# Seven products for a seventh pair, one weight sum by an adding DMA, and separate rooms, in a one-core encoder layer

## The chip, the cores and the metric

The kernel runs on one core of one Trainium2 chip. The metric is device time in microseconds (us): the time of one execution, as the median of several. A profiled execution also has a span, from its first to its last instruction.

The engines are PE (TensorE: matmuls, with PEld for the loads of its stationary operand), DVE (VectorE), ACT (ScalarE), POOL (GpSimd) and SP (SyncE). Almost all DMAs are issued from SP; DMAs that add what they bring to what lies at the destination are issued from POOL. Weights and activations are in float32.

## What the kernel computes

One layer of an encoder on 256 tokens of width 2048:

```python
h = x + 0.5 * rms_norm(swiglu(rms_norm(x, g1), w_gate1, w_up1, w_down1), p1)   # first FFN
u = rms_norm(h, g2); q, k, v, f, g = split(u @ w_in)
    # grouped-query attention on q, k, v (16 heads, 4 kv heads); a 2-D Fourier mix of f; gates from g
merged = sigmoid(g_A) * (attention @ w_attn_o) + sigmoid(g_B) * (fourier(f) @ w_fourier)
h = h + rms_norm(merged @ w_out, p2)
y = h + 0.5 * rms_norm(swiglu(rms_norm(h, g3), w_gate2, w_up2, w_down2), p3)   # second FFN

def swiglu(x, w_gate, w_up, w_down):
    return (silu(x @ w_gate) * (x @ w_up)) @ w_down
```

`w_gate` and `w_up` are 2048 x 5632 and `w_down` is 5632 x 2048; the two FFNs hold most of the arithmetic. The output has the shape of the input, in float32.

## The kernel before

**One product in three matmuls.** Every float32 operand is cut in two parts, `hi` (ACT copies it into a reduced format, L104) and `lo` (DVE subtracts `hi` from the source, L105). `mm3` (L108) multiplies two cut operands in three matmuls: hi by hi, lo by hi, hi by lo (L110 to L112). So each weight costs a load from HBM, an ACT copy and a DVE subtraction of the same size before PE may use it. "Split" below means this pair of instructions. A weight piece is 128 x 1024 (two rows of tiles of 128 x 512).

**The FFN.** The hidden width of 5632 is done in 11 blocks of 512 (`ffn`, L710). The first two blocks (`PLAIN` = 2) are straight products (`col_block`). The other nine go through `swiglu` (L558): the 16 tiles of the contraction, each 128 deep, are taken as eight pairs, and the 256 tokens are two tiles of 128. One pair has four activation tiles (two token tiles by two contraction tiles) and four weight tiles (gate and up, each by two contraction tiles): a 2 x 2 by 2 x 2 block product. Straight, this is eight products, 24 matmuls. By Strassen's scheme it is seven products of sums, 21 matmuls. `BY_SEVEN` (L48) names the pairs that go by seven: 0, 1, 2, 4, 5 and 6. Pairs 3 and 7 are straight.

**Left and right factors.** The seven left factors (sums of activation tiles) are made once for each FFN in `Forms.chunk` (L480) and kept. The right factors are sums of weights that are new for every block, and DVE makes them in `seven` (L602):

```python
minus(t[:, 0, :], ra[:, 1, :], ra[:, 0, :])           # L616; pairs in RAW_B8: one of 1024, L613
minus(t[:, 1, :], rb[:, 0, :], ra[:, 1, :])
b = ring(rb[:])                                       # split of 1024
minus(ra[:, 1, :], rb[:, 0, :], t[:, 0, :])           # L620
b = ring(h["t"][:])                                   # second(): split of 1024
minus(h["t"][:, 0, :], h["ra"][:, 1, :], h["rb"][:, 1, :])
line.feed(lambda: ring(h["ra"][:]), ...)              # split of 1024
line.feed(lambda: ring(h["t"][:, 0:1, :]), ...)       # split of 512
```

All subtractions go through the helper at L582. The sums after the products (`add`, L584, with its instruction at L587) put the seven accumulators together once in a block: eight additions and, at L599, two multiplications by the activated gate. `row_line` (L662) then multiplies a finished block by its rows of `w_down` (96 matmuls) while the next block is fed.

**The line and the ring.** `Line` (L525) is a hand-written order. `feed` appends a piece and, unless a piece with `hold` has stopped it, at once writes its preparation (load and split); `next` writes the matmuls of the oldest piece. So preparation runs up to `RING + RING_B8` = 8 pieces ahead of the matmuls, in split buffers (the ring): six in pool `wring` and two in `b8`. On DVE, ACT and PE this order is the order of execution. The order on SP and POOL is chosen by a scheduler at build time.

**Rooms.** Pool `b8` has 12 rooms of 8 KB per partition: left factors, two ring pieces, the raw 1 MB loads of pairs 0, 2, 4 and 6 (`RAW_B8`), layer inputs `u`, sums `y`, residual `h`, gains and the attention operands. Other raw pieces use five rooms of `wraw`. Pool `chunk` has three rooms for each of hi and lo of the hidden activations and serves as scratch.

**Handover and end.** `last_rows` (L261) does the last rows of a stage, then its norm (`PostNorm`) and the transposes of the next stage's input. The norm needs a reciprocal root, done on DVE in ten small instructions (`rsqrt_steps`, L151).

**Adding DMAs.** Two of four column groups of each `row_line` are added into `y` by a POOL DMA (L702), and the 16 pieces of the Fourier weights are folded by one each (L928).

Of the kernel before, what the change touches and what calls it, by code (L numbers as in the profile page):

```python
# [39 lines left out]
QSCALE = HD ** -0.5  # L40

# [17 lines left out]
def encoder_layer(  # L59
# [14 lines left out]
    b8 = pool("b8", B8)  # L74
    chunk = pool("chunk", CH)
# [11 lines left out]
    def big(name, dt=F32, shape=None):  # L87
        return b8.tile(shape or [P, D], dt, tag="b8", name=name)
# [38 lines left out]
    def pieces(src, spare=None):  # L127
# [4 lines left out]
        def part(k0):  # L132
            if spare in (None, "chunk"):
                return piece(src, k0, WP, (chunk, "ch_hi", "ch_lo") if spare else None)
            if not whole:
                for c in ("h", "l"):
                    shape = [P, CK, NB]
                    whole[c] = big("w" + c, F32R, shape)
# [12 lines left out]
    def rsqrt_steps(ssq, n, inv, name, mult=1.0, pre=None):  # L151

        up = (8.0 / 3.0 / mult) ** 2
        a, y, t, w, q, z, t2, w2, r = (small(name + c, n) for c in "aytwqzuvr")
        i = sm.tile([P, n], I32, tag="smi" + str(n), name=name + "i")
# [4 lines left out]
        yield r, V.tensor_scalar(out=i[:], in0=a[:].bitcast(I32), scalar1=1, scalar2=None, op0=ALU.logical_shift_right)  # L160
        yield r, V.tensor_scalar(out=y[:].bitcast(I32), in0=i[:], scalar1=-1.0, scalar2=float(0x5F3759DF),
                                 op0=ALU.mult, op1=ALU.add)
        yield r, V.tensor_tensor(out=t[:], in0=y[:], in1=y[:], op=ALU.mult)
        yield r, V.tensor_tensor(out=w[:], in0=t[:], in1=a[:], op=ALU.mult)
        yield r, V.scalar_tensor_tensor(out=q[:], in0=w[:], scalar=-10.0 / 3.0, in1=w[:], op0=ALU.add, op1=ALU.mult)
        yield r, V.scalar_tensor_tensor(out=z[:], in0=q[:], scalar=5.0, in1=y[:], op0=ALU.add, op1=ALU.mult)
        yield r, V.tensor_tensor(out=t2[:], in0=z[:], in1=z[:], op=ALU.mult)
        yield r, V.scalar_tensor_tensor(out=w2[:], in0=t2[:], scalar=-0.5 * 9.0 / 64.0, in1=a[:],
                                        op0=ALU.mult, op1=ALU.mult)
        yield r, V.scalar_tensor_tensor(out=r[:], in0=w2[:], scalar=1.5, in1=z[:], op0=ALU.add, op1=ALU.mult)  # L170
# [16 lines left out]
    def new_u(t):  # L187
        return tuple(big(f"u{c}{t}", F32R, [P, KD, P]) for c in "hl")
# [164 lines left out]
    def bcast(src, name):  # L353
        g = big(name)
        load(g[:], src.partition_broadcast(P))
        return g
# [4 lines left out]
    class PostNorm:  # L361
# [26 lines left out]
        def sums(self, t):  # L388
            up = (8.0 / 3.0 / self.half) ** 2
# [117 lines left out]
    def ring(src):  # L507
# [3 lines left out]
        if turn["more"] and i % 4 == 1:  # L511
            both = big("w2", F32R, [P, 2, WP, NB])
# [45 lines left out]
    def swiglu(line, forms, w, hs, behind={}):  # L558
# [4 lines left out]
        def mul(n, a, b, last=False):  # L563
            if n not in ps:
                ps[n] = ptr.tile([P, NB], F32, tag="tr", name="pc") if n in ("p5", "p7", "p1") else                     pmm.tile([P, NB], F32, tag="mm", name="pc")
            mm3(ps[n][:], *a, *b, n not in begun, last)
            begun.add(n)
# [4 lines left out]
        def plain(pair, i, *then, hold=False):  # L572
            def use(b):
                for t in range(NT):
                    for j in range(2):
                        k = 2 * pair + j
                        mul("gu"[i] + str(t), forms.plain[k][t], b[j], k == KD - 1)
# [3 lines left out]
        def minus(out, a, b):  # L581
            V.tensor_tensor(out=out, in0=a, in1=b, op=ALU.subtract)  # L582

        def add(out, a, b):  # L584
            if out not in x:
                x[out] = work(out)
            V.tensor_tensor(out=x[out][:], in0=ps[a][:], in1=x[b][:], op=ALU.add)  # L587
# [5 lines left out]
        def silu(t):  # L593
            g = x["x" + "13"[t]]
            A.activation(g[:], g[:], AF.Silu)

        def times(t):
            g, up = x["x" + "13"[t]], x["x" + "25"[t]]
# [3 lines left out]
        def seven(pair, between=None, *then):  # L602
# [4 lines left out]
            def first():  # L607
                t = chunk.tile([P, WP, NB], F32, tag=("ch_hi", "ch_lo")[BY_SEVEN.index(pair) % 2], name="t13")
                if turn["more"] and pair in RAW_B8:
                    four = big("raw4", F32, [P, 2 * WP, NB])  # L610
                    load(four[:], w[pair // 2].rearrange("p (i k c) -> p i k c", i=2, c=NB)[:, pair % 2])
                    ra, rb = four[:, 0:WP, :], four[:, WP:, :]
                    minus(t[:], four[:, 1:3, :], ra)  # L613
                else:
                    ra, rb = raw(pair, 0), raw(pair, 1)
                    minus(t[:, 0, :], ra[:, 1, :], ra[:, 0, :])  # L616
                    minus(t[:, 1, :], rb[:, 0, :], ra[:, 1, :])
                h.update(ra=ra, rb=rb, t=t)
                b = ring(rb[:])
                minus(ra[:, 1, :], rb[:, 0, :], t[:, 0, :])  # L620
                return b

            def second():
                b = ring(h["t"][:])
                minus(h["t"][:, 0, :], h["ra"][:, 1, :], h["rb"][:, 1, :])
                return b

            def two(n, a, m, b, last):
                def use(ws):
                    mul(n, a, ws[0], last)  # L630
                    mul(m, b, ws[1], last)
                return use

            line.feed(first, two("u0", s4, "g0", a12, False))
            line.feed(second, two("p5", s1, "p7", s3, end), hold=end)
            if between:
                between()
            line.feed(lambda: ring(h["ra"][:]), two("p1", a11, "p6", s2, end), *then[0:2], hold=end)
            line.feed(lambda: ring(h["t"][:, 0:1, :]), lambda ws: mul("g1", na22, ws[0]), *then[2:], hold=end)

        sums = [copy, lambda: add("x2", "p6", "x1"), lambda: add("x3", "p7", "x2"), lambda: add("x2", "p5", "x2"),
                lambda: add("x5", "p5", "x3")]
        gates = [lambda: add("x1", "g0", "x1"), lambda: add("x3", "g1", "x3"), lambda: silu(0), lambda: silu(1)]
        ups = [lambda: add("x2", "u0", "x2"), lambda: times(0), lambda: add("x5", "u1", "x5"), lambda: times(1)]
        for kg in range(KD // CK):
            a, b = 2 * kg, 2 * kg + 1
            if kg == KD // CK - 1:
                seven(a, None, *sums)
                if a in behind:
                    behind[a]()  # L650
                plain(b, 0, *gates, hold=True)
                plain(b, 1, *ups)
            elif b in BY_SEVEN:
# [4 lines left out]
            else:  # L658
                seven(a, lambda: plain(b, 0))
                plain(b, 1)  # L660

    def row_line(line, ch, w, rb, y, way, ahead):  # L662
# [4 lines left out]
        rooms = {(0, 0): (ptr, "tr"), (1, 0): (ptr, "tr"), (1, 1): (ptr, "tr")} if not first else {}  # L667
# [42 lines left out]
    def ffn(u, rs, wg, wu, wgu, wd, yname, tail, gate0, w_next=None, early=()):  # L710
# [29 lines left out]
        line = Line()  # L740
        end = []
        with tc.manual_schedule(engines={mybir.EngineType.DVE, mybir.EngineType.Activation, mybir.EngineType.PE}):
            for f in range(PLAIN, nblk + 1):
# [11 lines left out]
                if f < nblk:  # L755
                    hs = []
                    turn["more"] = True
                    swiglu(line, forms, wgu[f - PLAIN], hs, {
# [57 lines left out]
    def fourier_signs():  # L816
        alt = four["alt"] = xpool.tile([P, GROUPS // 2, NYR], F32R, tag="xt", name="alt")
        A.activation(alt[:].rearrange("p a b -> p (a b)"), constant(dft_ones[:, WE + P:], GROUPS // 2 * NYR)[:], AF.Copy)
        mid = four["mid"] = xpool.tile([NS, 2 * P + 2 * NYR], F32R, tag="xt", name="mid")
        mraw = work("mraw", [NS, 2 * P + 2 * NYR])  # L820
        load(mraw[:], dft_mid)
        A.activation(mid[:], mraw[:], AF.Copy)
# [566 lines left out]
```

## Time and profile before

| | before |
|---|---|
| median of 3 runs (lowest to highest) | 2001.39 us (2001.24 to 2002.6) |
| the profiled execution: time | 2003.93 us |
| the profiled execution: span | 2001.9 us |
| mean granted TensorE clock | 0.998 |
| PE busy | 1985.0 us (99%) |
| DVE busy | 1780.3 us (89%) |
| ACT busy | 1300.2 us (65%) |
| POOL busy | 84.4 us (4%) |
| DMA moved | 434.20 MB, mean 217 GB/s |

Busy time is the union of an engine's instructions in the records. Matmuls overlap in the records (a row lasts 0.39 us, the next one starts 0.23 us later), so a time on PE is worked out from start to start. An instruction row reads: start, duration, engine, line, operation, output<-input, shape, count and, in brackets, idle time before it with what ended that. In the rows, `wlo` or `w` from L105 is a DVE split, `pc` an accumulator of gate and up, `pr` one of the row products, `pt` a transpose. `w` alone is one of the two ring pieces in `b8`: every fourth piece.

### The profile page before, as it was taken

To read this page: it belongs to the slowest core of one execution; us is meant where nothing else is said; L and a number is where in the kernel's file an instruction comes from. 1 tells how busy PE (TensorE), PEld (TensorE's weight loads), DVE (VectorE), ACT (ScalarE), POOL (GpSimd) and SP (SyncE) were. 2 spreads that over 40 slices of the span, in tenths; PEclk is the share of its full clock that TensorE was granted. 3 is DMA by queue.
4 is the path that set the end of the run, shared out by engine and by line. 5 is a ranking of instruction groups with operands and counts; after the bars stand their busy time and mean duration, and the time that the engine had idled before them with its cause. 6 is when DMAs were issued, how large, how long until landed. Compare 5 with 4: busy or idle time off the path is not lost.

```text
span 2001.9 us, 25805 instructions
## 1 busy us (share of the span) xinstructions
PE 1985.0 (99%) x9146; PEld 1643.9 (82%) x9146; DVE 1780.3 (89%) x2352; ACT 1300.2 (65%) x1860; POOL 84.4 (4%) x94
## 2 busy tenths in 40 slices
PE   9999999999999999999999999999999999999998
PEld 7888888888888878888888888878888888888886
DVE  6999999999999888886877885878999999999996
ACT  7566766767666756556666564656677766777666
POOL 0000000000000010100000000000000000000002
PEclk9999999999999999999999999999999999999999
DMA  9657766677768796954555657565577766677683
GB/s 326 220 178 237 225 223 208 200 247 221 230 198 281 244 290 193 260 182 141 191 187 190 193 166 276 194 215 195 175 231 231 231 211 210 210 234 229 207 266 127
DMA packets 117585, 434.20 MB, mean 217 GB/s; under 512 B 12840, under 2 KB 18992, under 8 KB 106064
## 3 DMA queue, kind: packets, MB, share of 16 engines
q1 hardware_dynamic: 103888, 411.65, 60.6%
q0 software_dynamic: 13568, 20.91, 6.0%
q8 instruction: 71, 1.16, 0.2%
q14 instruction: 58, 0.48, 0.1%
HBM read 409.44 MB, written 6.29 MB: 208 GB/s over the span
## 4 chain that ended last, share of the span: by engine, by line
PE 92%; DVE 4%; DMA 2%; ACT 1%; issue 0%; SPq 0%; DVEq 0%; ACTq 0%
PE pc L111 18%; PE pc L112 18%; PE pc L110 18%; PE pr L112 10%; PE pr L111 10%; PE pr L110 10%; DVE wlo L105 2%; PE pt L180 1%; DMA raw<-in_w_fo 1%; PE pe L110 0%; PE pe L112 0%; PE pe L111 0%; DMA raw<-in_f_gu 0%; PE pt L1077 0%; PE pf L112 0%
## 5 line engine op out<-in xcount | busy, mean ns | idle before, releaser
L105 DVE TENSOR_TENSOR wlo<-raw,whi 128x1024 fp32r<-128x1024 f32 (+1 forms) x567 | 680.4, 1218 | 97.2 <-ACT whi L104 95.7
L104 ACT ACTIVATE whi<-raw 128x1024 fp32r<-128x1024 f32 (+1 forms) x567 | 586.0, 1052 | 253.9 <-PE pc L112 95.4
L111 PE MATMUL pc<-wlo,fh 128*128 128x512 f32 x738 | 287.5, 390 | 0.0
L112 PE MATMUL pc<-whi,fl 128*128 128x512 f32 x738 | 287.3, 389 | 0.0
L110 PE MATMUL pc<-whi,fh 128*128 128x512 f32 x738 | 287.1, 389 | 0.0
L110 PE MATMUL pc<-whi,uh 128*128 128x512 f32 x688 | 271.8, 396 | 1.0 <-ACT uh L834 1.0
L111 PE MATMUL pc<-wlo,uh 128*128 128x512 f32 x688 | 269.8, 392 | 2.0 <-DVE wlo L105 2.0
L112 PE MATMUL pc<-whi,ul 128*128 128x512 f32 x688 | 269.8, 392 | 0.0
L104 ACT ACTIVATE whi<-t 128x1024 fp32r<-128x1024 f32 (+1 forms) x198 | 171.6, 867 | 136.7 <-DVE t L582 125.5
L582 DVE TENSOR_TENSOR t<-raw 128x512 f32<-128x512 f32 (+1 forms) x252 | 208.9, 841 | 15.0 <-DMA raw<-in_f_gu 11.1
L110 PE MATMUL pr<-whi,hTh 128*128 128x512 f32 x544 | 213.4, 392 | 0.0
L112 PE MATMUL pr<-whi,hTl 128*128 128x512 f32 x544 | 211.8, 389 | 0.0
L111 PE MATMUL pr<-wlo,hTh 128*128 128x512 f32 x544 | 211.7, 389 | 0.0
L105 DVE TENSOR_TENSOR wlo<-t,whi 128x1024 fp32r<-128x1024 f32 (+1 forms) x198 | 193.4, 977 | 13.5 <-ACT whi L104 12.8
L104 ACT ACTIVATE w<-raw 128x1024 fp32r<-128x1024 f32 x144 | 152.0, 1055 | 42.0 <-DVE raw L582 35.3
L105 DVE TENSOR_TENSOR w<-raw,w 128x1024 fp32r<-128x1024 f32 x144 | 175.5, 1219 | 0.0
L111 PEld LDWEIGHTS pc<-wlo,fh 128*128 128x128 f32 x738 | 138.5, 188 | 29.5 <-DVE wlo L105 0.3
L110 PEld LDWEIGHTS pc<-whi,fh 128*128 128x128 f32 x738 | 138.5, 188 | 29.0
L112 PEld LDWEIGHTS pc<-whi,fl 128*128 128x128 f32 x738 | 138.5, 188 | 28.9
L111 PEld LDWEIGHTS pc<-wlo,uh 128*128 128x128 f32 x688 | 129.8, 189 | 28.9 <-DVE wlo L105 3.7
L110 PEld LDWEIGHTS pc<-whi,uh 128*128 128x128 f32 x688 | 129.9, 189 | 28.2 <-ACT uh L834 2.4
L112 PEld LDWEIGHTS pc<-whi,ul 128*128 128x128 f32 x688 | 129.6, 188 | 27.2 <-DVE ul L105 0.5
(360 smaller groups left out, 3185.1 us busy)
## 6 DMA issues: line engine op xcount, KB each, us to landing
raw<-in_f_down SPq DMA_DIRECT2D x176, 512.0 KB, 5.3
raw<-in_f_gu SPq DMA_DIRECT2D x144, 512.0 KB, 4.6
raw<-in_f_gu SPq DMA_DIRECT2D x72, 1024.0 KB, 7.7
raw<-in_w_in SPq DMA_DIRECT2D x112, 512.0 KB, 4.4
raw<-in_f_up SPq DMA_DIRECT2D x32, 512.0 KB, 4.8
raw<-in_w_ao SPq DMA_DIRECT2D x32, 512.0 KB, 4.3
raw<-in_w_out SPq DMA_DIRECT2D x32, 512.0 KB, 4.5
raw<-in_f_gate SPq DMA_DIRECT2D x31, 512.0 KB, 6.0
```

The costliest lines, as they stand in the source:

```text
L104: a = A.activation(hi, src, AF.Copy)
L105: v = V.tensor_tensor(out=lo, in0=src, in1=hi.bitcast(F32), op=ALU.subtract)
L110: T.matmul(ps, lh, rh, start=first, stop=False, skip_group_check=onto)
L111: T.matmul(ps, lh, rl, start=False, stop=False, skip_group_check=onto)
L112: return T.matmul(ps, ll, rh, start=False, stop=last, skip_group_check=onto)
L180: T.transpose(pt[:, j, :], src[:, j * P:(j + 1) * P], ident[:])
L582: V.tensor_tensor(out=out, in0=a, in1=b, op=ALU.subtract)
```

## The change

- **`BY_SEVEN` takes in pair 3.** Each of the 18 blocks (nine in each FFN) has seven pairs by seven products and one straight pair.
- **Another form of the seven products.** Before the products, DVE makes two subtractions for a pair, one of 512 and one of 1024 with a repeated operand; the third sum (first up tile plus first gate tile) is made by an adding DMA. The up half of a pair is loaded from SP into a room of the new pool `half`; then POOL issues a DMA that adds the first gate tile, 256 KB, onto its first tile; the gate half is loaded as an ordinary raw piece, so that the first gate tile comes twice. Class `Sums` fetches so up to three pairs ahead.
- **Order.** The fourth piece of a pair (`late`) is fed after the first piece of the next pair. The accumulator of up for the second token tile is gone: the straight pair adds onto the product `p5`. Seven additions close a block.
- **Rooms.** `b8` has 8 rooms; `rr` 2 rooms of 8 KB (the ring's two pieces, later the second token tile of `u`); `half` 6 rooms of 4 KB (the raw pairs, gains in halves, k, v and a Fourier operand, part of the last rows' weights); `chunk` 2 instead of 3. The left factors take three rests of `xpool` instead of one, so two Fourier constants move: `alt` to `const`, `mid` to a load and a copy at the start of the mixer.
- **Roots.** On one column, seven instructions instead of ten; on four columns, nine.

The diff, cut to its core:

```diff
-RAW_B8 = (0, 2, 4, 6)
-SPARE = (None, None, "chunk", "u")
+SPARE = (None, None, "chunk", "rr")
-B8 = 12
+B8 = 8
+RR = 2
+HALF = 6
-BY_SEVEN = (0, 1, 2, 4, 5, 6)
-CH = 3
+BY_SEVEN = (0, 1, 2, 3, 4, 5, 6)
+SUMS_AHEAD = 3
+CH = 2
...
             if spare in (None, "chunk"):
-                return piece(src, k0, WP, (chunk, "ch_hi", "ch_lo") if spare else None)
+                other = (chunk, "ch_hi", "ch_lo") if k0 == 0 else (half, "half", "half")
+                return piece(src, k0, WP, other if spare else None)
...
-        yield r, V.tensor_scalar(out=i[:], in0=a[:].bitcast(I32), scalar1=1, scalar2=None, op0=ALU.logical_shift_right)
-        yield r, V.tensor_scalar(out=y[:].bitcast(I32), in0=i[:], scalar1=-1.0, scalar2=float(0x5F3759DF),
-                                 op0=ALU.mult, op1=ALU.add)
-        yield r, V.tensor_tensor(out=t[:], in0=y[:], in1=y[:], op=ALU.mult)
-        yield r, V.tensor_tensor(out=w[:], in0=t[:], in1=a[:], op=ALU.mult)
+        yield r, V.tensor_scalar(out=y[:].bitcast(I32), in0=a[:].bitcast(I32), scalar1=-0.5,
+                                 scalar2=float(0x5F3759DF - 2 ** 31), op0=ALU.mult, op1=ALU.add)
+        def square_times_a(out, t, src):
+            if n == 1:
+                yield r, V.scalar_tensor_tensor(out=out[:], in0=src[:], scalar=src[:, 0:1], in1=a[:], op0=ALU.mult, op1=ALU.mult)
+            else:
+                yield r, V.tensor_tensor(out=t[:], in0=src[:], in1=src[:], op=ALU.mult)
+                yield r, V.tensor_tensor(out=out[:], in0=t[:], in1=a[:], op=ALU.mult)
+        yield from square_times_a(w, t, y)
...
         if turn["more"] and i % 4 == 1:
-            both = big("w2", F32R, [P, 2, WP, NB])
+            both = big("w2", F32R, [P, 2, WP, NB], rr)
...
+    class Sums:
+        def __init__(self, wgu, blocks):
+            self.todo = [(wgu[f], pair) for f in range(blocks) for pair in BY_SEVEN]
+            self.ready = []
+        def fetch(self):
+            w, pair = self.todo.pop(0)
+            src = w[pair // 2].rearrange("p (q i k c) -> p q i k c", q=2, i=2, c=NB)[:, pair % 2]
+            ra = small_room("ra", F32, [P, WP, NB])
+            load(ra[:], src[:, 1])
+            nc.gpsimd.dma_start(ra[:, 0, :], src[:, 0, 0], accum_op=ALU.add)
+            self.ready.append(ra)
+        def get(self):
+            while len(self.ready) <= SUMS_AHEAD and self.todo:
+                self.fetch()
+            return self.ready.pop(0)
...
             def first():
+                a = h["a"] = sums_.get()
+                b = ring(a[:])
+                V.tensor_tensor(out=a[:, 0, :], in0=a[:, 0, :], in1=a[:, 1, :], op=ALU.subtract)
                 return b
             def second():
+                b = h["b"] = raw(pair, 0)
+                r = ring(b[:])
+                V.tensor_tensor(out=b[:], in0=h["a"][:, 0:1, :].to_broadcast([P, WP, NB]), in1=b[:], op=ALU.subtract)
+                return r
+            line.feed(first, lambda ws: (mul("p5", s1, ws[0], end), mul("u0", s4, ws[1])))
+            while late:
+                late.pop()()
+            line.feed(second, lambda ws: (mul("p1", a11, ws[0], end), mul("g0", a12, ws[1])), *then[0:1], hold=end)
+            line.feed(lambda: ring(h["a"][:, 0:1, :]), lambda ws: mul("p6", s2, ws[0], end), *then[1:3], hold=end)
+            late.append(lambda: line.feed(lambda: ring(h["b"][:]),
+                                          lambda ws: (mul("p7", s3, ws[0], end), mul("g1", na22, ws[1], end)),
+                                          *then[3:], hold=end))
...
-        rooms = {(0, 0): (ptr, "tr"), (1, 0): (ptr, "tr"), (1, 1): (ptr, "tr")} if not first else {}
+        rooms = {(0, 0): (ptr, "tr"), (1, 0): (ptr, "tr")} if not first else {}
```

The rest of the diff gives every tile its new pool and splits the loads of the gains (`Gains`, 2 x 512 KB instead of 1 MB each).

More of the change, by code (lines that the diff above doesn't have):

```diff
@@ L74, in encoder_layer @@
     b8 = pool("b8", B8)
+    rr = pool("rr", RR)
+    half = pool("half", HALF)
     chunk = pool("chunk", CH)
@@ L137, in part @@
                     shape = [P, CK, NB]
[L138 removed]
+                    whole[c] = big("w" + c, F32R, shape, rr if spare == "rr" else b8)
             raw = wraw.tile([P, WP, NB], F32, tag="raw", name="raw")
@@ L351, in last_rows, with __init__, __getitem__ @@
         return ps
[L353 to L356, printed above, removed]
+    class Gains:
+        def __init__(self, src, name):
+            self.two = [small_room(name, F32, [P, D // 2]) for _ in range(2)]
+            for i, g in enumerate(self.two):
+                load(g[:], src[:, i * D // 2:(i + 1) * D // 2].partition_broadcast(P))
+        def __getitem__(self, at):
+            i, lo = divmod(at[1].start, D // 2)
+            return self.two[i][:, lo:lo + at[1].stop - at[1].start]
     def cbs(a, cb):
@@ L593, in silu, with seven @@
         def silu(t):
-            g = x["x" + "13"[t]]
+            g = x["x" + "12"[t]]
             A.activation(g[:], g[:], AF.Silu)
         def times(t):
-            g, up = x["x" + "13"[t]], x["x" + "25"[t]]
+            g, up = x["x" + "12"[t]], x["x" + "43"[t]]
             V.tensor_tensor(out=up[:], in0=up[:], in1=g[:], op=ALU.mult)
             hs.append(up)
-        def seven(pair, between=None, *then):
+        late = []
+        def seven(pair, *then):
             a11, a12, na22, s1, s2, s3, s4 = forms.seven[pair]
@@ L607, in first @@
             def first():
[L608 to L617, printed above, removed]
@@ L628, in two @@
[L628 to L639, printed above, removed]
@@ L645, in swiglu @@
+        sums = [copy, lambda: combine("x2", "p6", "x1", ALU.add), lambda: combine("x4", "p5", "x2", ALU.subtract)]
+        gates = [lambda: combine("x3", "p7", "x2", ALU.add), lambda: combine("x2", "g1", "x3", ALU.add),
+                 lambda: silu(0), lambda: silu(1)]
+        ups = [lambda: combine("x4", "u0", "x4", ALU.add), lambda: times(0),
+               lambda: combine("x3", "p5", "x3", ALU.subtract), lambda: times(1)]
         for kg in range(KD // CK):
@@ L647, in swiglu @@
             if kg == KD // CK - 1:
-                seven(a, None, *sums)
+                seven(a, *sums, *gates)
                 if a in behind:
                     behind[a]()
-                plain(b, 0, *gates, hold=True)
+                plain(b, 0, lambda: combine("x1", "g0", "x1", ALU.add), hold=True)
+                late.pop()()
                 plain(b, 1, *ups)
-            elif b in BY_SEVEN:
+            else:
                 seven(a)
@@ L894, in norm_rope @@
         return o
-    dps, dcs, odd, first, alt, mid = (four[n] for n in ("dps", "dcs", "odd", "first", "alt", "mid"))
-    kT = big("kT", F32R, [P, 2, 4, S])
-    vs = big("vs", F32R, [P, 2, NT, NB])
+    dps, dcs, odd, first, alt = (four[n] for n in ("dps", "dcs", "odd", "first", "alt"))
+    mm_ = xpool.tile([NYR, 3 * P + 2 * NYR], F32R, tag="xt", name="mid")
+    mid, mids = mm_[0:NS, 0:2 * P + 2 * NYR], mm_[:, 2 * P + 2 * NYR:]
+    mraw = work("mraw", [NS, 2 * P + 2 * NYR])
+    load(mraw[:], dft_mid)
+    kT = [small_room("kT" + c, F32R, [P, 4, S]) for c in "hl"]
+    vs = [small_room("vs" + c, F32R, [P, NT, NB]) for c in "hl"]
     ueo = [[big(f"u{n}{c}", F32R, [P, KD, P]) for c in "hl"] for n in "eo"]
@@ L1168, in encoder_layer @@
     kro = []
-    gate(10, mB, 0, between=[lambda b=b: fold_tokens(b) for b in range(1, 4)]
+    gate(10, mB, 0, between=[lambda b=b: fold_tokens(b) for b in range(1, 4)] + [lambda: A.activation(mid, mraw[:], AF.Copy)]
          + [lambda t=t: kro.append(norm_rope(pk, "k", t)) for t in range(NT)])
```

86 lines of the change are left out of this document (34 added, 52 removed).

## The prediction

> **What bounds the kernel now.** I read the page first, then the busy time of each engine by stretches, then the matmuls of one block of the FFN in order of time.
>
> ```profile
> span 2001.9 us, 25805 instructions
> PE 92%; DVE 4%; DMA 2%; ACT 1%; issue 0%; SPq 0%; DVEq 0%; ACTq 0%
> 174.61 0.87 PE pt L180 x8
> 236.84 0.87 PE pt L180 x8
> 270.20 0.39 PE L110 MATMUL pc<-w,fh 128*128 128x512 f32 x1
> 274.96 0.39 PE L110 MATMUL pc<-w,fh 128*128 128x512 f32 x1
> ```
>
> The chain that ended last is PE for 92% of the span. The transposes that come once in a block start 236.84 - 174.61 = 62.23 us apart: that is a block's period. The two matmuls each begin the piece of a pair that lies in one of the ring's special rooms, one pair (21 matmuls) apart: 4.76 / 21 = 0.2267 us for a matmul, whatever its row's 0.39 us says. A block has 6 x 21 + 2 x 24 + 96 = 270 matmuls, 61.2 us; with the transposes it fills the period. So PE runs at its own pace here, and a matmul less is 0.2267 us less, as long as the operands come.
>
> ```profile
> core 0: us, PE busy (x) PEld busy (x) DVE busy (x) ACT busy (x) POOL busy (x), PEclk, DMA share, GB/s
> 236.80:299.10 62.30, 62.30 (x281) 51.58 (x280) 60.42 (x69) 42.57 (x54) 3.52 (x5) 1.00 0.69 218
> 610.20:660.00 49.80, 49.80 (x224) 41.26 (x223) 48.00 (x56) 31.16 (x38) 0.92 (x2) 1.00 0.80 276
> 660.00:720.00 60.00, 58.55 (x273) 47.50 (x272) 51.18 (x84) 41.70 (x76) 4.39 (x4) 1.00 0.80 266
> ```
>
> Beside a full PE, DVE is busy 60.42 of 62.30 us. It is the second bound, with 1.9 us to spare, and whether a block gets shorter depends on whether DVE's work shrinks with PE's.
>
> **The matmuls.** Pair 3 goes from 24 matmuls to 21, in nine blocks of two FFNs: 18 x 3 x 0.2267 = 12.24 us. The new period would be 61.55 us. The new form of the products still has seven, and the straight pair, the row products and the transposes stay.
>
> **DVE's work.** Six rows give the subtractions, the additions and the pace.
>
> ```profile
> L582 DVE TENSOR_TENSOR t<-raw 128x512 f32<-128x512 f32 x180 | 121.1, 689 | 3.7
> L582 DVE TENSOR_TENSOR t<-raw 128x1024 f32<-128x1024 f32 x72 | 87.8, 1220 | 11.3 <-DMA raw<-in_f_gu 11.1
> L582 DVE TENSOR_TENSOR raw<-raw,t 128x512 f32<-128x512 f32 x108 | 73.9, 684 | 0.0
> L587 DVE TENSOR_TENSOR x<-pc,x 128x512 f32<-128x512 f32 x144 | 92.5, 683 | 1.2
> L486 DVE TENSOR_TENSOR un<-un,r 128x1024 f32<-128x1024 f32 x8 | 9.7, 1221 | 0.1
> 265.71 1.22 DVE L105 TENSOR_TENSOR w<-raw,w 128x1024 fp32r<-128x1024 f32 x1
> 266.84 0.68 DVE L105 TENSOR_TENSOR wlo<-t,whi 128x512 fp32r<-128x512 f32 x1
> 267.45 1.22 DVE L582 TENSOR_TENSOR t<-raw 128x1024 f32<-128x1024 f32 x1
> ```
>
> Start to start, an instruction of 1024 takes 266.84 - 265.71 = 1.13 us and one of 512 takes 0.61 us. By the counts, divided by 18, a block now has 10 + 6 = 16 subtractions of 512, four of 1024, and eight additions. Afterwards it has seven of 512, seven of 1024 and seven additions. Replacing a straight pair takes two splits of 1024 away and brings three of 1024 and one of 512. Net: of 1024, -4 + 7 - 2 + 3 = +4; of 512, -16 + 7 - 1 + 1 = -9. That is 4 x 1.13 - 9 x 0.61 = -0.97 us: DVE needs about 59.5 us in 61.55 and keeps 2.1 us to spare. The subtraction with a repeated operand is costed at 1.13 us because L486, with a repeated operand too, has the same 1221 ns as the plain ones. ACT gains one copy of 1024 and one of 512, bounded above by the 1.22 and 0.68 us of DVE's rows for the same sizes, so at most 1.9 us on 42.57: covered.
>
> **DVE's lead.** Within the sevens DVE is slower than PE, and lives on the lead it has won in the row products.
>
> ```profile
> 265.44 0.39 PE L110 MATMUL pc<-w,fh 128*128 128x512 f32 x1
> 259.17 1.22 DVE L105 TENSOR_TENSOR w<-raw,w 128x1024 fp32r<-128x1024 f32 x1
> 272.18 1.22 DVE L105 TENSOR_TENSOR w<-raw,w 128x1024 fp32r<-128x1024 f32 x1
> 254.39 1.23 DVE L582 TENSOR_TENSOR t<-raw 128x1024 f32<-128x1024 f32 x1 [0.54 <-DMA raw<-in_f_gu]
> ```
>
> The splits that end at 260.39, 266.93 and 273.40 are used at 265.44, 270.20 and 274.96: the lead goes from 5.05 to 3.27 to 1.56 us, about 1.75 us lost in a pair, since DVE takes 6.5 us for a pair and PE 4.76. The new form has one instruction of 512 less in such a pair: 5.9 us, a loss of 1.13. Now six pairs lose 10.5 us and the straight pair 3 gives back 24 x 0.2267 - 2 x 1.13 = 3.2, together 7.3; afterwards seven pairs lose 7.9 with nothing in between. The smallest lead goes from 1.56 to about 1.0 us, or 1.6 if the closing addition that DVE saves counts fully towards it. It stays above zero, so I cost it at nothing; if it is used up, each us that is missing in a block is 18 us in the end.
>
> **DMA, SP and POOL.** Each pair by seven now also moves 256 KB through an adding DMA.
>
> ```profile
> DMA  9999868048976204860576000588989986998799
> GB/s 294 390 278 192 191 221 287 18 79 311 387 248 248 87 0 79 316 279 0 161 242 253 18 0 0 169 279 269 248 242 348 453 348 161 316 306 229 308 383 229
> DMA packets 3518, 13.79 MB, mean 222 GB/s; under 512 B 394, under 2 KB 394, under 8 KB 3001
> q1 hardware_dynamic: 2885, 12.60, 59.5%
> q0 software_dynamic: 629, 1.14, 10.1%
> raw<-in_f_gu SPq DMA_DIRECT2D x144, 512.0 KB, 4.6
> y<-part POOLq DMA_DIRECT2D x32, 256.0 KB, 7.5
> DMA to landing us min/median/max: 6.4/7.9/12.1
> L702 POOL DMA_DIRECT2D y<-part x32: 847/941/1215, 168.2 to 610.3; - x32
> ```
>
> These are the DMAs of the block from 174.6 to 236.8 us, in 40 slices, and the nearest price of an adding DMA: POOL's sums onto `y`. In this block they cost 0.101 x 16 x 62.2 / 1.14 = 88 us of engine time for each MB; seven times 0.262 MB add 162 us to 0.70 x 16 x 62.2 = 697. That is 859 of 16 x 61.55 = 985 us, a share of 87%. The rate would be (13.79 + 1.83) / 61.55 = 254 GB/s, less than the 276 GB/s of the stretch from 610.2 us, where PE had no gap. So I take the throughput as sufficient. New waits: POOL's add waits for the up half to land, with later adds and the row products' sums queued behind it; ACT's split of the sum waits for the add, with all splits, and DVE, behind it; SP's load waits for a room of `half`, with the raw loads behind it. One sum needs 4.6 us to load, 0.94 to issue and 7.9 (12.1 at worst) to land: 13.4 to 17.6 us. Six rooms are 28.6 us of PE at 4.76 a pair, and about 6 us of that a room is in use, so 22 us are there. POOL goes from four issues in a block to eleven, 10.3 us of 61.55. These cost nothing on the path; their upper bound is the second rival.
>
> **The rest.** Three steps of the root go. At the end of the kernel nothing covers them:
>
> ```profile
> 1993.36 0.15 DVE L160 TENSOR_SCALAR ci<-ca 128x1 int32<-128x1 int32 x1
> 1993.55 0.15 DVE L161 TENSOR_SCALAR cy<-ci 128x1 int32<-128x1 int32 x1
> 1993.73 0.48 DVE L163 TENSOR_TENSOR ct<-cy 128x1 f32<-128x1 f32 x1
> 1994.26 0.16 DVE L164 TENSOR_TENSOR cw<-ct,ca 128x1 f32<-128x1 f32 x1
> ```
>
> A step is 0.19 us from start to start, the third row 0.53. Three steps are 0.57 us, 0.91 if the long one goes; I take 0.57. At the two handovers the same 0.57 us lies on a path where PE has up to 1.45 us of gaps (660 to 720 us): a gain between 0 and 1.1, and I count 0. Against it, the smaller pools can hold things up: with two rooms in `chunk`, the last rows' third weight waits until the row products before it are done, and `h` waits for rooms of `b8`. A late split costs 1.22 us on DVE and no more on ACT, and the first two column groups of the last rows cover it with 24 x 0.2267 = 5.4 us: 0, and 2.4 for each handover if that cover is gone. The moved constant is one small load and one copy, the halves of the gains one more issue each, ahead of weights that SP loads in advance: 0.
>
> **The sum.** 12.24 + 0.57 = 12.8 us off the profiled span: 2001.9 becomes 1989.1. The profiled execution took 2003.93 us, 2.0 more than its span, and the median of the three runs is 2.5 below it at 2001.39; both offsets should stay, so the median becomes **1988.6 us**.
>
> **Rivals.** *DVE's lead runs out.* For it: only about 1 us is left, and DVE did wait 0.54 us for a weight in the block shown. Against it: DVE's total falls more than PE's. If waits take the lead and 0.4 us more in each block, 7 us come back: 1995.8, between 1991 and 2001 for 0.15 to 0.7 us. Chance 0.14.
>
> *DMA becomes the bound, and the kernel slower.* Many slices of the block show a nine, and the share has to go from 0.70 to 0.87. If no more than 0.80 were to be had, the most in a stretch with PE full, a block would take 859 / (16 x 0.80) = 67.1 us, 4.9 longer: 2089. It decides from a ceiling of 859 / (16 x 62.23) = 0.863 downwards. Against it: slices with a nine carry anything from 161 to 453 GB/s, so a nine is not full throughput. Chance 0.09.
>
> *POOL and DVE shut each other out.* Were each of the seven issues to hold DVE for its 0.94 us, DVE would lack 6.6 - 2.1 = 4.5 us in a block, which becomes 66.05 us: 2001.39 + 18 x 3.82 = 2070. The trace speaks against it:
>
> ```profile
> 292.48 1.75 POOL L702 DMA_DIRECT2D y<-part  x2 [54.99 <-ACT part L701]
> 292.00 1.22 DVE L582 TENSOR_TENSOR t<-raw 128x1024 f32<-128x1024 f32 x1
> 293.13 1.22 DVE L105 TENSOR_TENSOR w<-raw,w 128x1024 fp32r<-128x1024 f32 x1
> 294.27 0.68 DVE L582 TENSOR_TENSOR raw<-raw,t 128x512 f32<-128x512 f32 x1
> ```
>
> DVE keeps its 1.13 us through two issues. Chance 0.02. The Trainium skill ("SBUF — State Buffer", section "Who interferes with whom") has a rule of this kind: a DVE instruction with two inputs in SBUF and a GpSimd instruction that reads SBUF exclude each other for the whole of the first one. By that rule, if issuing reads SBUF, the time would be this rival's; the four rows show no such hold.
>
> *The handovers lose their cover*: 2 x 2.4 us, 1993.4. Chance 0.07.
>
> **How the numbers follow.** The forecast has 0.68. A measurement of this kernel can tell about 0.2%, 4 us, from no change. Below 1997.4 lie the forecast, the handovers and about half of the first rival: 0.82. Within 0.2% lies the rest of the first rival: 0.07. Above lie the second and third: 0.11. The range begins at 1985, with the root's 1.1 us at the handovers, the long step's 0.34 and some 2 us of gaps closed elsewhere; it ends at 1998, past the handovers and half of the first rival.
>
> **What would show it.** Right: the eight transposes of a block 61.55 us apart; PE without gaps in the blocks; DVE near 59.5 us of it; DMA share at 0.8 to 0.9; adds landing in 7 to 12 us; roots of seven rows. Wrong: PE idle released by DVE splits in the last pairs (first rival); ACT waiting for the sum of a pair in most pairs (second); DVE rows much longer than 1.22 us beside POOL's issues (third); gaps of 2 us about each handover (fourth).

## The result, and the profile after

| | before | after |
|---|---|---|
| median of 4 runs each, on the same chip | 2001.99 us (2001.24 to 2003.48) | 2126.24 us (2116.86 to 2129.34) |
| ratio, 95% interval | | 1.0613 [1.0596, 1.063] |
| span of the profiled execution | 2001.9 us | 2125.4 us |
| mean granted TensorE clock | 0.998 | 0.979 |

I had forecast 1988.6 us; the kernel became 6.1% slower. These are the page of the changed kernel, then its waits, PE's among them (what waited for what: us in total, times, the longest), then its time by stretches, with the columns as before.

```profile
span 2125.4 us, 26315 instructions
PE 2024.8 (95%) x9092; PEld 1652.8 (78%) x9092; DVE 1777.7 (84%) x2230; ACT 1334.2 (63%) x1906; POOL 193.6 (9%) x220
PE 55%; DVE 23%; DMA 10%; issue 9%; ACT 3%; SPq 0%; DVEq 0%; ACTq 0%; POOLq 0%
```
```profile
PE pc L118 <- DVE x L625: 83.3, 18, 5.8
ACT whi L112 <- DMA raw<-in_f_down: 45.0, 19, 5.2
ACT w L112 <- DMA raw<-in_f_down: 39.4, 9, 5.4
```
```profile
core 0: us, PE busy (x) PEld busy (x) DVE busy (x) ACT busy (x) POOL busy (x), PEclk, DMA share, GB/s
322.10:391.30 69.20, 64.22 (x276) 51.88 (x275) 60.23 (x63) 43.87 (x55) 9.54 (x11) 0.98 0.78 220
365.00:370.00 5.00, 2.10 (x10) 1.37 (x8) 1.69 (x2) 1.54 (x2) 0.88 (x1) 1.00 1.00 346
370.00:375.00 5.00, 3.10 (x7) 2.49 (x8) 4.76 (x8) 1.76 (x3) 0.00 (x0) 0.70 0.95 328
```

PE is 55% of the chain, no longer 92%. In this longer block DVE does not lack time in sum: 60.23 of 69.20 us. What is new is one wait, exactly once in each of the 18 blocks: PE's first matmul of a straight piece (L118) waits for a closing addition of DVE (L625), 83.3 us in all. And ACT waits 28 times for a weight of the row products (`in_f_down`). The block's end shows how the two hang together. PE, in order of time:

```profile
322.10 1.03 PE L192 MATMUL pt<-ident,x 128*128 128x128 f32 x8
366.70 0.40 PE L120 MATMUL pc<-whi,frest 128*128 128x512 f32 x1
371.90 0.78 PE L118 MATMUL pc<-whi,frest 128*128 128x512 f32 x1 [4.81 <-DVE x L625]
372.90 0.63 PE L120 MATMUL pc<-whi,frest 128*128 128x512 f32 x1
373.33 0.63 PE L118 MATMUL pc<-whi,frest 128*128 128x512 f32 x1
375.43 0.39 PE L120 MATMUL pr<-w,hTl 128*128 128x512 f32 x1
391.35 1.03 PE L192 MATMUL pt<-ident,x 128*128 128x128 f32 x8
```

SP's queue, ACT and DVE at the same place:

```profile
361.48 9.40 SPq L90 DMA_DIRECT2D raw<-in_f_down  x6
368.21 1.06 ACT L112 ACTIVATE whi<-raw 128x1024 fp32r<-128x1024 f32 x1 [4.47 <-DMA raw<-in_f_down]
360.23 3.49 DVE L113 TENSOR_TENSOR wlo<-raw,whi 128x1024 fp32r<-128x1024 f32 x3
364.78 1.22 DVE L113 TENSOR_TENSOR wlo<-raw,whi 128x1024 fp32r<-128x1024 f32 x1
369.30 1.23 DVE L113 TENSOR_TENSOR wlo<-raw,whi 128x1024 fp32r<-128x1024 f32 x1 [3.31 <-ACT whi L112]
370.44 3.99 DVE L625 TENSOR_TENSOR x<-pc,x 128x512 f32<-128x512 f32 x6
```

Read backwards: the straight pair now adds onto `p5`, so PE may multiply the second token tile of its up half only when DVE has read `p5` in a closing addition (370.44). On DVE that addition stands behind the split of a row weight that is prepared ahead (369.30); the split waits for ACT's copy, the copy for the load, and the load went out only at 361.48, some 6.7 us before it was used. The load was late for want of a room. The first of the three splits that begin at 360.23 ends 1.22 us later and gives its raw piece's room back, and the load goes out 0.03 us after that. The gate half of each pair is now an ordinary raw piece that keeps one of `wraw`'s five rooms until its late split, and the two straight pieces and two row weights fill the others.

The block's 391.35 - 322.10 = 69.25 us are 7.70 more than the 61.55 I had forecast. The idle stretch is 371.90 - 366.70 - 0.23 = 4.97 us. The eight matmuls behind it take 375.43 - 371.90 = 3.53 us, not 1.81: 1.72 more, since they start 0.43 us apart, not 0.23, and the granted clock is 0.70 in that stretch. About 1.0 us is left, and it lies in the sevens:

```profile
341.65 0.69 DVE L113 TENSOR_TENSOR w<-ra,w 128x512 fp32r<-128x512 f32 x1
347.64 0.69 DVE L113 TENSOR_TENSOR w<-ra,w 128x512 fp32r<-128x512 f32 x1
353.64 0.68 DVE L113 TENSOR_TENSOR w<-ra,w 128x512 fp32r<-128x512 f32 x1
359.63 0.69 DVE L113 TENSOR_TENSOR w<-ra,w 128x512 fp32r<-128x512 f32 x1
```
```profile
345.43 0.39 PE L118 MATMUL pc<-w,fh 128*128 128x512 f32 x1
350.19 0.39 PE L118 MATMUL pc<-w,fh 128*128 128x512 f32 x1
354.95 0.39 PE L118 MATMUL pc<-w,fh 128*128 128x512 f32 x1
360.00 0.39 PE L118 MATMUL pc<-w,fh 128*128 128x512 f32 x1
```

DVE splits one such piece in each pair every 5.99 us, and PE uses one every 4.76. The lead is 345.43 - 342.34 = 3.09 us, then 1.86, then 0.63; at the last pair the split ends at 360.32, after PE has come to the piece, and PE's step is 360.00 - 354.95 = 5.05 us. The lead is used up: PE loses 0.26, 0.25 and 0.44 us at the splits of the pieces that it begins at 356.99, 360.00 and 360.94, 0.95 us in all.

The eight periods between an FFN's nine groups of transposes took 497.8 us in the first FFN before and 553.7 after, and 498.5 and 553.7 in the second. That is 111 of the 123.5 us. The stretch up to the first transposes, which holds the first block of this kind, has 8.1 more, the one between the last transposes of the first FFN and the first ones of the second 4.6.

### The profile page after: what moved, and what is told of

Read it like the earlier page. It is cut to its first block, busy times and chain, and to the rows that moved or that the text cites. A ratio compares the mean times of both kernels' runs of the same rounds, so it can differ in the third digit from the quotient of the medians.

```text
span 2125.4 us, 26315 instructions
## 1 busy us (share of the span) xinstructions
PE 2024.8 (95%) x9092; PEld 1652.8 (78%) x9092; DVE 1777.7 (84%) x2230; ACT 1334.2 (63%) x1906; POOL 193.6 (9%) x220
## 4 chain that ended last, share of the span: by engine, by line
PE 55%; DVE 23%; DMA 10%; issue 9%; ACT 3%; SPq 0%; DVEq 0%; ACTq 0%; POOLq 0%
DVE wlo L113 16%; PE pr L118 9%; PE pr L119 9%; PE pr L120 9%; PE pc L118 8%; PE pc L119 8%; PE pc L120 8%; DMA raw<-in_f_down 6%; DVE w L113 4%; DMA ra<-in_f_gu 3%; ACT whi L112 2%; DVE x L625 1%; PE pt L192 1%; ACT w L112 0%; PE pe L118 0%
## 5 line engine op out<-in xcount | busy, mean ns | idle before, releaser
L113 DVE TENSOR_TENSOR wlo<-raw,whi 128x1024 fp32r<-128x1024 f32 (+1 forms) x612 | 733.4, 1218 | 159.1 <-ACT whi L112 158.0
L112 ACT ACTIVATE whi<-raw 128x1024 fp32r<-128x1024 f32 (+1 forms) x612 | 633.1, 1053 | 316.3 <-PE pc L120 108.4
L118 PE MATMUL pc<-whi,uh 128*128 128x512 f32 x688 | 271.4, 395 | 0.9 <-ACT uh L857 0.9
L118 PE MATMUL pc<-whi,fh 128*128 128x512 f32 x657 | 256.0, 390 | 0.3 <-DVE hTl L113 0.3
L120 PE MATMUL pc<-whi,fl 128*128 128x512 f32 x657 | 256.1, 390 | 0.0
L589 POOL DMA_DIRECT2D ra<-in_f_gu x126 | 109.0, 865 | 1335.2 <-DVE h L424 444.5
L113 DVE TENSOR_TENSOR wlo<-ra,whi 128x1024 fp32r<-128x1024 f32 (+1 forms) x180 | 182.7, 1032 | 52.2 <-ACT whi L112 52.2
L118 PE MATMUL pr<-whi,hTh 128*128 128x512 f32 x544 | 217.8, 400 | 0.0
L112 ACT ACTIVATE whi<-ra 128x1024 fp32r<-128x1024 f32 (+1 forms) x180 | 160.3, 905 | 43.2 <-DVE ra L650 21.8
L112 ACT ACTIVATE w<-raw 128x1024 fp32r<-128x1024 f32 x99 | 104.5, 1056 | 129.5 <-DVE raw L656 64.8
L656 DVE TENSOR_TENSOR raw<-ra,raw 128x1024 f32<-128x1024 f32 x126 | 154.4, 1225 | 4.3
L118 PE MATMUL pc<-whi,frest 128*128 128x512 f32 x162 | 73.7, 455 | 83.3 <-DVE x L625 83.3
L118 PEld LDWEIGHTS pc<-whi,uh 128*128 128x128 f32 x688 | 129.7, 188 | 27.5 <-ACT uh L857 2.2
L113 DVE TENSOR_TENSOR w<-raw,w 128x1024 fp32r<-128x1024 f32 x99 | 120.7, 1220 | 30.0 <-ACT w L112 29.8
```

Source lines behind the costliest of these rows:

```text
L112: a = A.activation(hi, src, AF.Copy)
L113: v = V.tensor_tensor(out=lo, in0=src, in1=hi.bitcast(F32), op=ALU.subtract)
L118: T.matmul(ps, lh, rh, start=first, stop=False, skip_group_check=onto)
L120: return T.matmul(ps, ll, rh, start=False, stop=last, skip_group_check=onto)
L589: nc.gpsimd.dma_start(ra[:, 0, :], src[:, 0, 0], accum_op=ALU.add)
L656: V.tensor_tensor(out=b[:], in0=h["a"][:, 0:1, :].to_broadcast([P, WP, NB]), in1=b[:], op=ALU.subtract)
```

## The experiments

The expectations call the theories by letters. A: the shared accumulator `p5` lets PE wait for DVE's late additions, the late row weight behind it. A2, formed later: beside that, DVE's lead runs out. B: the added DMA load makes the transfers late (B2 for what remained). C: DVE's lead in the sevens is used up, and DVE alone sets the pace; A2 takes this up again for the part that A leaves. Each kernel is the changed one with the edit shown, if no other is named; "before" ran beside each, at 2001.1 to 2002.6 us.

**An accumulator of its own for up (`e1`).**

```diff
-                        n = ("g0", "g1", "u0", "p5")[NT * i + t]
+                        n = ("g0", "g1", "u0", "u1")[NT * i + t]
...
-               lambda: combine("x3", "p5", "x3", ALU.subtract), lambda: times(1)]
+               lambda: combine("x3", "p5", "x3", ALU.subtract), lambda: combine("x3", "u1", "x3", ALU.add), lambda: times(1)]
...
-        rooms = {(0, 0): (ptr, "tr"), (1, 0): (ptr, "tr")} if not first else {}
+        rooms = {(0, 0): (ptr, "tr"), (1, 0): (ptr, "tr"), (1, 1): (ptr, "tr")} if not first else {}
```

> The changed kernel, but up for the second token tile has an accumulator of its own again (one more addition of 512 on DVE in a block, 0.6 us). Theory A (the matmuls that add onto p5 wait for a DVE addition that stands behind the split of a late row weight; 5 us of PE idle in a block, and 1.7 to 2.8 us at a lower clock after it): the gap of 5 us and the slow matmuls go, DVE still waits some 3 us in a block for the late load, so the block falls from 69.9 to between 61.6 and 63.5 us: 1990 to 2025. Theory B (the adding DMAs make all loads late): the loads stay late and the block stays above 66 us: 2080 or more. Theory C (DVE's lead in the sevens is used up and DVE sets the pace): one more addition makes it no better: 2110 to 2140.

Measured: 2061.38 us, ratio 1.0294 [1.0269, 1.0319]. With an accumulator of its own the kernel is 65 us faster, so C fails: an addition more for DVE did not leave the time as it was. But some 60 us stay, more than A allowed for. A part of the wait only moved, to the row products:

```profile
PE pr L118 <- ACT x L629: 27.2, 16, 3.1
ACT whi L112 <- DMA raw<-in_f_down: 46.8, 14, 6.2
```

The weight comes as late as before, and now PE waits for ACT, whose copy of `p1` is queued behind it.

**Rooms for the row weights (`e2`).** The straight pair's raw pieces go into `half`; two rooms of `wraw` come free.

```diff
-            line.feed(lambda: ring(raw(pair, i)[:]), use, *then, hold=hold)
+            def ready():
+                a = small_room("raw", F32, [P, WP, NB])
+                load(a[:], w[pair // 2].rearrange("p (i k c) -> p i k c", k=WP, c=NB)[:, pair % 2 * 2 + i])
+                return ring(a[:])
+            line.feed(ready, use, *then, hold=hold)
```

> The changed kernel, but the two raw pieces of the straight pair are loaded into rooms of half, so that two more row weights fit into wraw ahead of the closing additions. Theory A: the row weight is no longer late, DVE reaches the closing additions about 3.3 us earlier, PE's gap falls from 5 to some 1.5 us and with it most of the low clock: a block of 64 to 66 us, 2030 to 2070. Theory B: loads stay late, 2100 or more. Theory C: no change, 2110 to 2140.

Measured: 2041.17 us, 1.0191 [1.0174, 1.0208]. PE's wait for the closing additions:

```profile
PE pc L118 <- DVE x L630: 27.2, 18, 3.3
```

It falls from 83.3 to 27.2 us, its longest from 5.8 to 3.3, and the time by 85: more than the 56 of waiting, since the slow matmuls go too (the granted clock is 0.998).

**Both (`e3`).**

> Both edits together: own accumulator, and the straight pair's raw pieces in rooms of half. Theory A: no gap and no late row weight, PE at its own pace of 61.6 us in a block: 1986 to 1996, faster than the kernel before. Theory B: 2080 or more. Theory C: 2110 to 2140.

Measured: 2015.49 us, 1.0061 [1.0043, 1.0078]. Theory A misses by 20 us: with both mended the blocks take 62.6 to 63.0 us, and one 63.8, not 61.55. What is left of PE's waits is small, frequent, and for splits:

```profile
PE pc L119 <- DVE wlo L113: 4.9, 23, 0.6
```

**The adding DMAs left out (`e4`).** POOL's issue in `Sums.fetch` goes; the up tile takes the place of the sum, so this kernel does not compute the layer.

```diff
-            nc.gpsimd.dma_start(ra[:, 0, :], src[:, 0, 0], accum_op=ALU.add)
```

> The changed kernel without the adding DMA of the weight sum (the sum is left out: the up tile alone takes its place); loads, splits, matmuls and rooms are the same. Theory A: the DMA's load is not the cause, the gap on p5 stays: 2100 to 2130. Theory B: the loads come on time and most of the 125 us is gone: below 2040. Theory C: no change, 2110 to 2140.

Measured: 2115.92 us, 1.0569 [1.0553, 1.0585]; 434.21 MB moved, as before the change. The added transfers and issues explain some 10 of 124 us.

**Less for DVE, with both mends (`e5`).** On top of `e3`, the subtraction of 512 in `first()` goes; the sum takes the place of the difference, so this kernel and the two others without it (`e10`, `e11`) do not compute the layer.

```diff
-                V.tensor_tensor(out=a[:, 0, :], in0=a[:, 0, :], in1=a[:, 1, :], op=ALU.subtract)
```

> The kernel with own accumulator and the straight pair's raw pieces in half, and without the subtraction of 512 in first() (the difference of the first two sums is left out, the sum itself takes its place): DVE has 0.6 us less in each of seven pairs, everything else is the same. Theory A2 (what is left after the two mends, a block of 62.6 instead of 61.55 us, is DVE's lead that runs out at the last pair): the gaps of PE before the last pair's pieces go and the block falls to 61.6 us: 1993 to 2000. Theory B2 (what is left comes from the fuller DMA): the block stays at 62.6: 2012 to 2018.

Measured: 1990.28 us, 0.9937 [0.992, 0.9953]. The transposes:

```profile
235.27 1.03 PE L192 MATMUL pt<-ident,x 128*128 128x128 f32 x8
296.84 1.03 PE L192 MATMUL pt<-ident,x 128*128 128x128 f32 x8
```

They are 61.57 us apart, against a forecast of 61.55. Seven instructions of 0.61 us less on DVE in a block bring what the fewer matmuls were to bring, with every adding DMA in place. So B2 falls, and what was left lies with DVE. DVE's own waits from 1470 to 1850 us, some six blocks, in `e3` and then in `e5`:

```profile
DVE wlo L113 <- ACT whi L112: 5.9, 13, 0.7
DVE wlo L113 <- ACT whi L112: 29.5, 24, 2.1
```

In `e3` DVE waits about 1 us in a block of 62.6: with the small gaps between its instructions its work fills some 61.6 us, as much as PE's matmuls. So `e5` does not tell a lead that runs out within the block from a total that has come up to PE's; it took from both.

**Pair 3 straight again, with both mends (`e6`).** The change stays, but for `BY_SEVEN = (0, 1, 2, 4, 5, 6)`: as many matmuls as before.

> Both mends, but pair 3 by straight products again: the new products, the adding DMAs (six in a block), pools and roots stay, and PE has its 270 matmuls. Theory A2: the straight pair in the middle gives DVE's lead back, the block is PE's 62.2 us: 1998 to 2005, so that the seventh pair by itself, at 2015, makes the kernel slower. Theory B2: DMA still adds 256 KB in six pairs, the block stays at 62.6 or more: 2010 to 2020.

Measured: 1997.22 us, 0.9978 [0.9969, 0.9988]; 62.10 us a block. It computes the whole layer and beats both kernels, the one before by 4.8 us, of which the roots alone bring 2.5 (`e7`). With a straight pair in the middle PE no longer waits for DVE in the blocks. This fits a lead that is given back there, but DVE also has less to do: it is busy 57.2 us in a block, against 60.8 in `e3`.

**The roots alone (`e7`).** The kernel before with the roots of the change.

> The kernel before with the shorter roots alone. All theories: three steps of 0.19 us less at the end and at the two handovers: 0.5 to 1.7 us faster than before, 1999.5 to 2002, which the times alone can hardly tell; the end of the profile shows seven steps instead of ten.

Measured: 1999.51 us, 0.9985 [0.9976, 0.9995]: 2.5 us less. At the end the steps from L159 to the root take 2.00 us, not 2.34. In the profiles, whose spans differ by 4.2 us, 3.7 lie between the last transposes of the first FFN and the first ones of the second: 789.56 us, against 793.25 before, where PE waited 1.02 and 0.41 us for splits (at 712 and 715 us) that it does not wait for here.

**The up half of the straight pair behind pair 3 (`e8`).** On top of `e3`, to refill the lead in the middle without giving up the seventh pair. The hold and the closing additions move ahead with it.

```diff
...
+                if b == 3:
+                    plain(KD // 2 - 1, 1)
```

> Both mends, and the up half of the straight pair moved behind pair 3, with the hold from the last pair's first piece on. Theory A2: the lead grows by 1.6 us in the middle, PE has no gap before the last pair, and the block falls to 61.6 to 61.9 us: 1990 to 2002. Theory B2: 2012 or more. If the closing additions come too late for the row products' PSUM rooms, PE waits there instead: 2010 to 2030.

Measured: 2041.01 us, 1.0197 [1.0179, 1.0215]: worse than `e3`, and beyond the ranges of A2 and of the wait for PSUM rooms. PE's waits for splits in the sevens, 4.9 us in `e3`, are down to 0.2, but waits have come up behind the sevens, in the row products:

```profile
PE pr L118 <- ACT pr L718: 21.8, 16, 2.5
PE pr L119 <- DVE wlo L113: 8.2, 9, 1.2
PE pr L119 <- DVE w L113: 7.8, 9, 1.2
```

With only the gate half left at the end, less covers the closing additions; whether this is why the row products wait, no run shows.

**The third pieces out of the ring (`e9`).** On top of `e3`, their splits go into scratch rooms, so that the ring's eight reach further ahead.

```diff
+                hi, lo = workr("t3h"), workr("t3l")
+                split(hi[:], lo[:], h["a"][:, 0, :])
```

> Both mends (own accumulator, the straight pair's raw pieces in half), and the split of a pair's third piece, 512 wide, goes into two rooms of wk instead of a ring room, in all pairs but the last; the ring then holds eight other pieces, so that DVE may run up to two pieces further ahead. DVE's work is the same. Theory A2 (DVE's lead runs out at the last pair because the ring ends it too early at the start): the lead starts up to 1.4 us larger, the gaps before the last pair go, and the block falls from 62.6 to 61.6 to 62.0 us: 1990 to 2003. If DVE's total in a block is the limit instead, the block stays at 62.6: 2010 to 2018.

Measured: 2019.12 us, 1.0089 [1.0073, 1.0105]. It tells little: the scratch rooms are shared with sums on their way to `y`, and so ACT and DVE have new waits.

```profile
1794.72 0.69 DVE L113 TENSOR_TENSOR t3l<-ra,t3h 128x512 fp32r<-128x512 f32 x1 [2.29 <-DMA yf<-part]
```

**The shared accumulator with less for DVE (`e10`).** `e2` without the subtraction.

> The shared accumulator of the changed kernel, the straight pair's raw pieces in half, and no subtraction of 512 in first() (the difference of the first two sums is left out, the sum itself takes its place). Theory A2 (the shared accumulator costs PE time only because DVE comes to the closing additions without a lead): with 4 us more of lead PE no longer waits for them: 1988 to 2000. If the shared accumulator costs 1.5 us in a block whatever the lead, as between 2041 and 2015: 2012 to 2022.

Measured: 1990.77 us, 0.9945 [0.9932, 0.9959]. Where weights come in time and DVE has a lead, adding onto `p5` costs next to nothing: PE waits once for a closing addition, 2.1 us.

**The change as it is, with less for DVE (`e11`).** Only the subtraction goes.

> The changed kernel as it is (shared accumulator p5, straight pair's raw pieces in the row weights' rooms), only without the subtraction of 512 in first(); the difference is left out of the computation. It closes the table: so far this edit was made only where the late load had been mended. Theory (DVE's lead is the first cause, the late load and the shared accumulator only make its loss dearer): DVE has 7 x 0.61 = 4.3 us a block more, its splits free the rooms earlier, the row weight is loaded in time: 1988 to 2005, and PE's waits for the closing additions fall from 83 us to under 15. Rival (the late load stands by itself, since the rooms are too few whatever DVE does): the 56 us that mending the load took from those waits, with the slow matmuls behind them, stay: 2050 to 2080. Between 2010 and 2045 both count.

Measured: 2050.12 us, 1.0238 [1.022, 1.0256]. The time is at the rival's lower edge, 45 us above my theory's range; 76 us of `after` went with DVE's work, 49 over the kernel before stay. PE's wait, and the load behind it (SP's queue; ACT):

```profile
PE pc L118 <- DVE x L625: 40.6, 16, 3.5
```
```profile
342.26 9.82 SPq L90 DMA_DIRECT2D raw<-in_f_down  x6
349.41 1.06 ACT L112 ACTIVATE whi<-raw 128x1024 fp32r<-128x1024 f32 x1 [4.19 <-DMA raw<-in_f_down]
```

DVE has 4.3 us a block less to do, and the weight still arrives 7 us after a room was free to ask for it. The late load is a cause by itself.

**The subtraction on POOL (`e12`).** On top of `e3`; nothing is left out.

```diff
-                V.tensor_tensor(out=a[:, 0, :], in0=a[:, 0, :], in1=a[:, 1, :], op=ALU.subtract)
+                nc.gpsimd.tensor_tensor(out=a[:, 0, :], in0=a[:, 0, :], in1=a[:, 1, :], op=ALU.subtract)
```

> The version with its own up accumulator and the straight pair's raw pieces in rooms of half, with the subtraction of 512 in first() done by POOL and not by DVE; nothing is left out. POOL's other subtraction-like rows of 128x512 took 1078 ns. Theory (DVE's lead): DVE has 4.3 us a block more, as where the subtraction was left out, and the time is the same as there: 1988 to 1995, faster than both kernels. Rival (POOL and DVE shut each other out): each POOL row holds DVE for its 1.08 us, 7.6 us a block in place of 4.3, so DVE is 3.3 us a block worse off than with its own subtraction: 18 x 3.3 = 59 us on 2015, 2060 to 2080, with POOL's rows or DVE's beside them much longer than 1.08 and 1.22 us. Third: POOL's subtraction stands behind adding DMAs that wait for their loads, and DVE waits for it: 2000 to 2040, with DVE waits that POOL ends.

Measured: 2078.04 us, 1.0382 [1.0368, 1.0396], near the 2074 that the rival gives (2015 + 59). Two rows of POOL, then two of DVE:

```profile
323.24 2.19 POOL L655 TENSOR_TENSOR ra<-ra 128x512 f32<-128x512 f32 x1 [3.15 <-DVE wlo L113]
329.68 2.19 POOL L655 TENSOR_TENSOR ra<-ra 128x512 f32<-128x512 f32 x1 [1.88 <-DVE wlo L113]
```
```profile
323.06 3.45 DVE L113 TENSOR_TENSOR wlo<-raw,whi 128x1024 fp32r<-128x1024 f32 x2
329.50 3.46 DVE L113 TENSOR_TENSOR wlo<-raw,whi 128x1024 fp32r<-128x1024 f32 x2
```

Two splits take 2.35 us in `after`; beside a POOL subtraction they take 1.1 more, and POOL's row takes 2.19 us. The 1078 ns in the expectation are a mean over two shapes; the six POOL rows of 128x512 in the kernel before take 1309 ns on average. So beside each other POOL's row is 0.9 us longer and DVE's two splits are 1.1 us longer. The subtraction costs DVE 1.1 us on POOL and 0.61 on DVE itself: 7 x (1.1 - 0.61) = 3.4 us a block and 62 in all, where 2078.04 - 2015.49 = 62.5 came. DVE waits for POOL's results themselves for 9.4 us only in the whole run, so the third theory is a small part at most.

The medians together, in us; "less for DVE" is without the subtraction:

| accumulator | straight pair's loads | as it is | less for DVE |
|---|---|---|---|
| `p5`, shared | in `wraw` | 2126.24 (after) | 2050.12 (`e11`) |
| its own | in `wraw` | 2061.38 (`e1`) | not run |
| `p5`, shared | in `half` | 2041.17 (`e2`) | 1990.77 (`e10`) |
| its own | in `half` | 2015.49 (`e3`) | 1990.28 (`e5`) |

## Why the prediction was wrong, point by point

- **The matmuls** were right. With the disturbances gone, a block takes 61.57 us and the kernel 1990, as worked out (61.55 and 1988.6).
- **DVE's work** in sum was near: 60.2 us busy in a block, where I had 59.5. But the 2.1 us to spare were not there. In `e3` DVE is busy 60.8 us and waits about 1 us of 62.6; the small gaps between its instructions take the rest. And a total below PE's says nothing of the order within a block.
- **DVE's lead** is the first step that failed: "It stays above zero, so I cost it at nothing". A pair takes DVE 5.99 us, where I had 5.9, so it loses 1.23 us and not 1.13; over seven pairs that is 0.7 us of the 1.0 I thought left. The measured lead of -0.3 us is another 0.6 below, which I can't place. What DVE lacks costs 25 us by itself (`e3` against `e5`); how much of it is the lead at its lowest point and how much the total, the runs don't tell. My first rival had the mechanism, but priced it at 7 us.
- **The waits that I costed at nothing** are the second, and the larger one. I named the sum in the diff (onto `p5`) without asking what PE would wait for there, and counted the rooms of `half` but not those of `wraw`, where a pair's gate half now stays for long. With less for DVE, the late load costs 2050.12 - 1990.77 = 59 us (`e11` against `e10`, both with the shared accumulator), and the shared accumulator without the late load 0.5 (`e10` against `e5`). With DVE's work as it is, mending the load alone brings 85 and the accumulator alone 65, both together 111: they lie on one path.
- **The lower clock** was not in my sum at all. It is 1.72 us in the block shown, behind 5 us of idle PE. The Trainium skill ("TensorE: Matmul & The Clock Gate", "Part 1: The HAM clock gate") gives 426.7 ns between such matmuls for a throttled array, and some 3.4 us until it is released; the 0.43 us and 3.5 us here agree.
- **The DMA bound** did not come: the share is 0.78 in the block shown, with the transfers spread over a longer block. In `e10`, whose block is 61.6 us, it is 0.85 in one block and 0.91 in the next, about the 0.87 worked out, and PE has no gap there. The slices with a nine in my block carry 192 to 453 GB/s, not from 161: that slice has an eight.
- **The root** was over-rated at the kernel's end: 0.34 us came and not 0.57, since one of the new steps takes 0.67 us (`e7`). At the first handover I counted nothing, and the profiles of `e7` suggest that it gained there.
- **POOL and DVE**: beside the adds' issues DVE's rows keep their length, 1.22 to 1.23 us for 1024, and the subtraction with a repeated operand costs what I took, 1225 ns. But as soon as POOL computes, the two do hold each other up (`e12`). The Trainium skill ("SBUF — State Buffer", "Who interferes with whom") says so of a DVE instruction with two inputs in SBUF and a GpSimd instruction that reads SBUF; the 1.1 us in `e12` agree.
- **The handovers** are not settled. The stretch from the last transposes of the first FFN to the first ones of the second is 4.6 us longer after the change, but it holds a block whose closing addition PE waits 5.6 us for; in `e3` it is 3.2 longer, with a wait of 2.0 us in the attention. In `e5` it is 1.0 shorter than before, but 2.6 longer than in `e7`, which has the same roots and the old rooms. So the smaller pools may have cost some of what the fourth rival priced; no run tries them alone.

Also open: a form with seven pairs by seven that leaves DVE enough lead. `e8`, `e9` and `e12` are three that don't.

## What to carry to other kernels

Where an engine feeds another from a lead, work out the lead at its lowest point, row by row, and not the totals; when that comes out near zero, price its loss. When a result is added onto an accumulator that another engine still reads, everything queued on that engine ahead of the read comes onto the path. Count prefetch rooms by how long each piece stays in its room, not by how many pieces there are.

## What of the hardware was not expected

The adding DMAs from HBM land sooner than the sums from SBUF by which I had priced them. Issues with size and median us to landing, then POOL's and DVE's groups, in `after`, and the DMA queue of POOL's issues (packets, MB, share of the 16 engines) before and after:

```profile
ra<-in_f_gu POOLq DMA_DIRECT2D x126, 256.0 KB, 5.6
y<-part POOLq DMA_DIRECT2D x32, 256.0 KB, 7.9
```
```profile
L589 POOL DMA_DIRECT2D ra<-in_f_gu x126 | 109.0, 865 | 1335.2 <-DVE h L424 444.5
L656 DVE TENSOR_TENSOR raw<-ra,raw 128x1024 f32<-128x1024 f32 x126 | 154.4, 1225 | 4.3
```
```profile
q0 software_dynamic: 13568, 20.91, 6.0%
q0 software_dynamic: 31712, 53.95, 15.4%
```

They land in 5.6 us where the sums take 7.9; in `e3`, with shorter blocks, in 7.0 where the sums take 9.7. In engine time they are not cheaper: by the queue's shares of the two spans, the 33.04 MB that came to it take about 100 us for each MB (an estimate; the shares are rounded), where I had 88. And a pause of PE can cost more than itself: 5 us of idle cost 1.7 us of slow matmuls behind it. In `e2`, where no wait for a closing addition is longer than 3.3 us, the mean granted clock is 0.998.
